# Joined products for both halves of the softmax weights, and the forget gate inside the value projection

## The chip, the core and the metric

The kernel runs on one core of one Trainium2 chip. The metric is the device time of one execution in microseconds (us), lower is better. Times below are medians of runs; the rows come from one more execution that the hardware profiler recorded.

## What is computed

One decoder layer over 2048 tokens of width 1024, in float32. Three sub-layers, each `x <- x + RMSNorm(f(RMSNorm(x)))`: a token mixer with a causal convolution (width 31) beside attention with a forget gate, a cross-attention to 256 memory tokens, and a squared-ReLU MLP of width 4096. The change touches the attention of the mixer:

```
log_f = log_sigmoid(f_logit + b_forget)            # 8 heads, one column each of the input projection
cum = cumsum(log_f, axis=1)
logits = q @ k.T * scale + cum[q] - cum[k]         # causal, 8 heads of 64, in blocks of 128 queries
p = softmax(logits)
out = p @ v
```

## The kernel before

A float32 product that must be exact enough is made of float32r parts: every operand `x` is split into a high half (a rounded copy, made by ACT) and a low half (`x - high`, made by DVE), and a product of two split operands takes three matmuls: high by high, high by low, low by high. `mm3` (lines 160 to 167) issues them; `split` (134) makes the halves; `weight` (144) loads a weight tile and splits it.

The tokens go through in four chunks of 512. `mix_in` (336) handles 1024 tokens (two chunks) at a time: the gated linear unit and the keys and queries of each 128 channels, and then the values, in two column halves `b` of 256 (four heads of 64 each), 128 tokens at a time. Results go to DRAM. `attend` (492) runs the attention of one chunk: 8 heads, each in two blocks of 256 queries. For a block, `scores` (539) makes the logits in pieces of up to 512 keys (line 560, 561), adds the bias and takes the row maximum on DVE, and exponentiates on ACT. `values` (580) then walks over the keys in pairs of 128: four transpositions on PE (line 594) of the weights into one PSUM bank `pt`, the split of it into `pp` (high by ACT, low by DVE, line 598), and, one pair behind, the products with the values (line 610) into `o`. The value tile holds, for 128 keys, 64 high and 64 low columns, so that one matmul yields 128 rows: `v_high` times the weights and `v_low` times the weights. Each key block takes two matmuls of 256 columns, one with the high half of the weights and one with the low; the second block of the last pair, which only 128 of the queries may see, takes 128 columns. At the end ACT copies one half of the rows of `o` and DVE adds the other (lines 616, 617).

The forget gate (`gate`, 458) is made early, after the first 128 channels of `mix_in`: 32 matmuls of 512 columns for each 1024 tokens (lines 467, 468) with a stationary operand of 40 columns, then a chain on ACT and DVE over tiles of 8 partitions by 1024 tokens, with a running sum over the tokens at its end. The sums go to DRAM (`dnc`), and `attend` reads them back for every head, spread over 128 partitions (`bias`).

What runs beside what: `drive` (932) interleaves two streams of work. The main stream is `mix_in` for the first and second 1024 tokens and then the four MLPs; the side stream is the attention, output projection and cross-attention of chunk 0, 1, 2, 3. The convolution (480 taps of `acc`, one DVE instruction each, and 16 first taps) comes from a background list between them; what is left of a chunk's taps when its output projection needs them is flushed. A scheduler then orders the instructions of every engine by priority, and the numbers in `SCHED` (57) set ratios and leads: `r0`, `a1`, `m0` to `m2` the share of side work, `a0`, `b1`, `bm` that of the convolution, `hw`, `hb`, `hs`, `hm` leads of weights, background, side and main.

Of the kernel before, what the change touches and what calls it, by code (L numbers as in the profile page):

```python
# [10 lines left out]
F32 = mybir.dt.float32  # L11
F32R = mybir.dt.float32r
# [6 lines left out]
P = 128  # L19
# [6 lines left out]
NH = 8  # L26
# [27 lines left out]

SCHED = dict(hw=135, hb=117, hs=62.8, hm=39.2, r0=0.243, a0=0.35, a1=1.16, b1=0.186, m0=0.85, m1=0.986, m2=1.12,
           bm=0.161, y1=3.05, y2=2.3, y3=2.97, y4=1.95)


class Engine:
# [19 lines left out]
class Trunk:  # L81
# [130 lines left out]
    def setup(self):  # L212
        nc, i = self.nc, self.i
        ct = lambda shape, name, dt=F32: self.cpool.tile(shape, dt, name=name)
        self.ident = ct([P, P], "ident")
        make_identity(nc, self.ident)
        self.ones = ct([P, 1], "ones")
        self.v.memset(self.ones, 1.0)
        self.mean_d, self.mean_c = ct([P, 1], "mean_d"), ct([P, 1], "mean_c")
        self.v.memset(self.mean_d, 1.0 / D)  # L220
        self.v.memset(self.mean_c, 1.0 / CCH)
        self.eps = ct([P, 1], "eps")
        self.v.memset(self.eps, EPS)
# [4 lines left out]
        self.bf = ct([NH, 1], "bf")  # L228
        self.wf = ct([P, KT, 32 + NH], "wf", F32R)
        self.carry = ct([NH, 1], "carry")  # L230
# [12 lines left out]
        self.d_x1 = [self.dram([P, KT, TC], name="dx1") for _ in range(NCH)]  # L243
        self.d_x2 = [self.dram([P, KT, TC], name="dx2") for _ in range(NCH)]

    def setup_late(self):
        nc, i = self.nc, self.i
        self.load(self.cw, i["conv_w"])
        self.load(self.cvec, i["cvec"])
        self.load(self.bf, i["b_forget"])  # L250
# [4 lines left out]
        self.v.memset(self.wf.bitcast(F32), 0.0)  # L255
        raw = self.tile("vs", [P, KT, NH], name="wfraw")
        self.load(raw, i["w_f"])
        yield 1
        self.a.copy(self.wf[:, :, 0:NH], raw)
        self.v.tensor_tensor(out=self.wf[:, :, 32 : 32 + NH], in0=raw,  # L260
                                in1=self.wf[:, :, 0:NH].bitcast(F32), op=ALU.subtract)


    def mem_load(self):
# [71 lines left out]
    def mix_in(self, h, ht, late, after):  # L336

        nc, i = self.nc, self.i
        for t in range(4):
            glu, key, query = self.glu(h, t, ht), self.qk(h, t, ht, 12), self.qk(h, t, ht, 8)  # L340
            if t == 0:
                for _ in range(4):
                    yield next(glu)
                next(late, None)
                yield next(key)
                for _ in late:
                    pass
                yield next(key)
            yield from glu
            yield from key  # L350
            yield from query
            if t == 0:
                yield from self.gate(h, ht)
        for b in range(2):
            wv = []
            for q in range(2):
                wv.append([self.tile("mu", [P, 4, 256], F32R, name="wv") for _ in range(2)])
                self.weight(i["w_v"][b, q], [4, 256], wv[q])
            wk = [(wv[k // 4][0][:, k % 4], wv[k // 4][1][:, k % 4]) for k in range(KT)]
            for t in range(8):  # L360
                sl = slice((t % 4) * P, (t % 4 + 1) * P)
                ps = self.ps("mm")
                self.mm3(ps[:, :256], [(a[:, sl], bb[:, sl]) for a, bb in ht[t // 4]], wk)
                v = self.tile("ms", [P, 4, 2, DH], F32R, name="v")
                pv = ps[:, :256].rearrange("p (h d) -> p h d", d=DH)
                self.split(v[:, :, 0], v[:, :, 1], pv)
                self.store(
                    self.d_v[h][4 * b : 4 * b + 4, :, t].rearrange("h p d -> p h d"),
                    v.bitcast(F32).rearrange("p h l d -> p h (l d)"))
                yield 2.6  # L370
                if b == 1 and t == 3:
                    for _ in after:
                        pass
# [81 lines left out]
                              scale=self.cvec[:, 1, t : t + 1])  # L455
            yield SCHED["y4"]

    def gate(self, h, ht):

        nc = self.nc  # L460
        W = HALF
        z, e, u, ln = [self.tile("mu", [NH, W], name="gate") for _ in range(4)]
        for j in range(2):
            ps = self.ps("mm")
            for k in range(KT):
                xh, xl = ht[j][k]
                nc.tensor.matmul(ps[: 32 + NH], self.wf[:, k], xh, start=k == 0, stop=False)
                nc.tensor.matmul(ps[: 32 + NH], self.wf[:, k], xl, start=False, stop=k == KT - 1)
            sl = slice(j * TC, (j + 1) * TC)
            self.a.copy(e[:, sl], ps[32 : 32 + NH])  # L470
            self.v.scalar_tensor_tensor(
                out=z[:, sl], in0=ps[:NH], scalar=self.bf, in1=e[:, sl], op0=ALU.add, op1=ALU.add)
            yield 3.5
# [4 lines left out]
        self.a.activation(ln, u, AF.Ln)  # L478
        self.v.reciprocal(u, u)
        self.mul(e, e, u)  # L480
        self.v.tensor_tensor(out=ln, in0=ln, in1=e, op=ALU.subtract)
        self.v.tensor_scalar(out=z, in0=z, scalar1=0.0, scalar2=None, op0=ALU.min)
        self.v.tensor_tensor(out=ln, in0=ln, in1=z, op=ALU.subtract)
        self.v.tensor_tensor_scan(
            out=u, data0=self.ones[:NH, 0:1].to_broadcast([NH, W]), data1=ln,
            initial=0.0 if h == 0 else self.carry, op0=ALU.mult, op1=ALU.add)
        if h == 0:
            self.a.copy(self.carry, u[:, W - 1 : W])
        self.store(self.d_nc[h], u)


    def attend(self, c):
# [87 lines left out]
    def values(self, c, hd, b, prow, v):  # L580
# [1 line left out]
        L = c * TC + (b + 1) * QB  # L582
        e = hd % 2
        nk = L // P
        o = self.ps("o")[:, :QB]
        prev = None
        for k0 in range(0, nk + 2, 2):
            cur = None
# [10 lines left out]
                cur = (k0, pp)  # L599
            if prev is not None:  # L600
                g, pp = prev
                order = [(0, 0), (0, 1), (1, 0), (1, 1)]
                if g == nk - 2:
                    order = [(0, 0), (1, 0), (1, 1), (0, 1)] if g == 0 else order[2:] + order[:2]
                for n, (k, l) in enumerate(order):
                    if g + k == nk - 1:
                        out, rhs = o[:, P:], pp[:, l, QB : QB + P]
                    else:
                        out, rhs = o, pp[:, l, k * QB : (k + 1) * QB]
                    nc.tensor.matmul(out, v[:, g + k], rhs, start=g == 0 and n == 0, stop=g == nk - 2 and n == 3)  # L610
# [473 lines left out]
```

## Time and profile before

| what | value |
|---|---|
| median of 3 runs | 2839.58 us (2838.35 to 2840.03) |
| the profiled execution: time, span | 2844.77 us, 2843.0 us |
| PE busy | 2774.1 us (98%), 13922 matmuls |
| DVE busy | 1966.3 us (69%) |
| ACT busy | 1380.7 us (49%) |
| POOL busy | 207.2 us (7%) |
| mean granted TensorE clock | 0.993 of full speed |

The profiled execution is 5.2 us (0.18%) above the median. Busy time is the time with at least one instruction of the engine in flight; matmuls overlap, so what one costs is read from the distance between the starts of neighbours. An idle stretch is put down to the instruction whose end released it.

### The profile page before, as it was taken

The numbers are of one execution on the slowest core, as the hardware profiler recorded it, in microseconds if no ns is written. First come the engines' busy times: TensorE is split into PE (matmuls) and PEld (weight loads), VectorE is DVE, ScalarE is ACT, GpSimd is POOL, SyncE is SP. The second block draws the span as 40 slices with busy tenths as digits, with TensorE's granted clock in tenths as the row PEclk, the third lists the DMA queues.
The fourth block names the chain that finished last, engine by engine and source line by source line (L and its number), as shares of the span: only waits on it lengthen the run. The fifth ranks groups of instructions, "written<-read, shape, count | busy, mean of one in ns | idle before, by whom it ended". The sixth has DMA issues, their size and how long they took to land.

```text
span 2843.0 us, 37221 instructions
## 1 busy us (share of the span) xinstructions
PE 2774.1 (98%) x13922; PEld 2303.9 (81%) x13922; DVE 1966.3 (69%) x3521; ACT 1380.7 (49%) x2164; POOL 207.2 (7%) x367
## 2 busy tenths in 40 slices
PE   7999999999999999989999999999999999999997
PEld 5889778888888887878888888878887888888887
DVE  8878896669787676888886645876665555844436
ACT  5333654345654445556554445655555445543332
POOL 0010300001110000021100001011100000000000
PEclk9999999999999999999999999999999999999999
DMA  5366645456544344456453435354524342342332
GB/s 170 116 221 167 172 131 164 141 163 199 153 135 130 128 136 145 149 151 175 133 147 115 149 107 167 127 180 146 151 93 135 119 148 97 130 145 97 97 96 82
DMA packets 141045, 398.32 MB, mean 140 GB/s; under 512 B 15248, under 2 KB 37904, under 8 KB 136000
## 3 DMA queue, kind: packets, MB, share of 16 engines
q1 hardware_dynamic: 99952, 262.40, 29.0%
q0 software_dynamic: 40912, 133.54, 16.3%
q8 instruction: 110, 1.80, 0.3%
q14 instruction: 71, 0.58, 0.1%
HBM read 330.68 MB, written 65.20 MB: 139 GB/s over the span
## 4 chain that ended last, share of the span: by engine, by line
PE 78%; DMA 5%; issue 5%; DVE 4%; ACT 2%; POOL 1%; SPq 0%; POOLq 0%; DVEq 0%; ACTq 0%
PE mm L165 17%; PE mm L166 17%; PE mm L167 17%; PE sc L167 4%; PE sc L165 4%; PE sc L166 4%; PE o L610 4%; PE pt L594 3%; PE sc L560 2%; PE sc L561 2%; DMA bias<-dnc 1%; DMA rb<-drs 1%; DMA cu<-du 1%; DVE yacc L73 1%; DVE acc L73 1%
## 5 line engine op out<-in xcount | busy, mean ns | idle before, releaser
L73 ACT CAST wh<-wr 128x1024 fp32r<-128x1024 f32 x282 | 296.5, 1052 | 705.6 <-PE mm L166 640.8
L165 PE MATMUL mm<-h,wh 128*128 128x512 f32 x1504 | 597.8, 398 | 6.2 <-ACT h L73 2.6
L166 PE MATMUL mm<-h,wh 128*128 128x512 f32 x1504 | 595.3, 396 | 1.7 <-DVE h L73 1.7
L167 PE MATMUL mm<-h,wl 128*128 128x512 f32 x1504 | 596.5, 397 | 0.0
L73 DVE TENSOR_TENSOR wl<-wr,wh 128x1024 fp32r<-128x1024 f32 x282 | 345.3, 1224 | 276.4 <-ACT wh L73 274.9
L165 PE MATMUL mm<-hid,wh 128*128 128x512 f32 x992 | 395.4, 399 | 0.6 <-DVE yacc L73 0.6
L167 PE MATMUL mm<-hid,wl 128*128 128x512 f32 x992 | 392.9, 396 | 0.0
L166 PE MATMUL mm<-hid,wh 128*128 128x512 f32 x992 | 392.1, 396 | 0.0
L73 DVE SCALAR_TENSOR_TENSOR acc<-cu,convw,acc 128x512 f32<-128x512 f32 x480 | 357.0, 748 | 5.9
L165 PEld LDWEIGHTS mm<-h,wh 128*128 128x128 f32 x1504 | 284.0, 189 | 65.7 <-ACT h L73 3.0
L166 PEld LDWEIGHTS mm<-h,wh 128*128 128x128 f32 x1504 | 283.9, 189 | 60.4 <-DVE h L73 3.2
L167 PEld LDWEIGHTS mm<-h,wl 128*128 128x128 f32 x1504 | 283.7, 189 | 58.1
L73 DVE TENSOR_TENSOR yacc<-mm,yacc 128x512 f32<-128x512 f32 (+1 forms) x232 | 154.9, 669 | 159.4 <-PE mm L167 158.1
L73 DVE TENSOR_TENSOR pp<-pt,pp 128x512 fp32r<-128x512 f32 (+1 forms) x288 | 186.8, 656 | 71.7 <-ACT pp L73 70.2
L73 ACT CAST pp<-pt 128x512 fp32r<-128x512 f32 (+1 forms) x288 | 159.4, 560 | 130.1 <-PE pt L594 123.7
L165 PEld LDWEIGHTS mm<-hid,wh 128*128 128x128 f32 x992 | 186.4, 188 | 39.9 <-DVE yacc L73 1.7
L167 PEld LDWEIGHTS mm<-hid,wl 128*128 128x128 f32 x992 | 186.5, 188 | 38.0 <-issue 0.5
L166 PEld LDWEIGHTS mm<-hid,wh 128*128 128x128 f32 x992 | 186.6, 188 | 36.8 <-DVE hid L73 0.2
L594 PE MATMUL pt<-ident,prow 128*128 128x128 f32 x1088 | 200.0, 276 | 3.5 <-ACT prow L73 3.5
L73 ACT ACTIVATE prow<-prow,mx 128x128 f32<-128x128 f32 (+15 forms) x128 | 154.2, 1205 | 79.9 <-DVE mx L73 77.2
L73 DVE CUSTOM_DVE_ANT_0 prow<-sc,bias 128x512 f32<-128x512 f32 (+3 forms) x288 | 166.8, 596 | 34.3 <-PE sc L561 29.5
L610 PE MATMUL o<-pp,vv 128*128 128x256 f32 (+1 forms) x832 | 179.7, 300 | 8.8 <-DVE pp L73 8.1
(234 smaller groups left out, 4569.4 us busy)
## 6 DMA issues: line engine op xcount, KB each, us to landing
wr<-in_w_up_dram SPq DMA_DIRECT2D x128, 512.0 KB, 3.6
wr<-in_w_down_dram SPq DMA_DIRECT2D x128, 512.0 KB, 3.5
wr<-in_w_in_dram SPq DMA_DIRECT2D x32, 512.0 KB, 4.2
q<-dq POOLq DMA_DIRECT2D x64, 256.0 KB, 5.7
wr<-in_w_out_dram SPq DMA_DIRECT2D x32, 512.0 KB, 3.5
dx<-y SPq DMA_DIRECT2D x16, 1024.0 KB, 4.2
bias<-dnc POOLq DMA_DIRECT2D x32, 512.0 KB, 5.7
x<-in_x_dram POOLq DMA_DIRECT2D x12, 1024.0 KB, 6.3
```

Of the source, the lines that this page charges most:

```text
L73: ins = op(*args, **kw)
L165: mm(ps, ah, bh, start=first and j == 0, stop=False)
L166: mm(ps, ah, bl, start=False, stop=False)
L167: mm(ps, al, bh, start=False, stop=last and j == n - 1)
L560: nc.tensor.matmul(ps[:, :w], q[:, 0, qs], ks[:, k0 : k0 + w], start=True, stop=False)
L561: nc.tensor.matmul(ps[:, :w], q[:, 1, qs], ks[:, k0 : k0 + w], start=False, stop=True)
L594: nc.tensor.transpose(pt[:, at : at + P], prow[t][:, (k0 + k) * P : (k0 + k + 1) * P], self.ident)
L610: nc.tensor.matmul(out, v[:, g + k], rhs, start=g == 0 and n == 0, stop=g == nk - 2 and n == 3)
```

## The change

It has three parts. First, `values` makes one matmul of each key block for both halves of the weights: the moving operand is the high and the low half side by side (512 columns), the result goes to two halves of the PSUM bank, and one more DVE addition joins them. The columns of the value tile are laid out so that the high half of the values stands on the same rows for both, and the product of the low halves is not added up any more. Second, the eight columns of the forget gate become columns 256 to 263 of the value projection's moving operand for the first four heads; the gate's chain then works on 128 partitions by 64, and the running sum is made by small matmuls with triangular constants. The chain comes at the end of the first half of the value projection. Third, eight numbers of `SCHED` differ, and the scheduler orders all engines anew.

```diff
-SCHED = dict(hw=135, hb=117, hs=62.8, hm=39.2, r0=0.243, a0=0.35, a1=1.16, b1=0.186, m0=0.85, m1=0.986, m2=1.12,
-           bm=0.161, y1=3.05, y2=2.3, y3=2.97, y4=1.95)
+SCHED = dict(hw=153, hb=124, hs=61, hm=42.2, r0=0.254, a0=0.346, a1=1.16, b1=0.186, m0=0.85, m1=0.986, m2=1.12,
+             bm=0.102, y1=3.12, y2=2.3, y3=2.97, y4=1.95)
...
+        for t in (self.tri, self.same, self.prior):
+            nc.gpsimd.memset(t, 1.0)
+        sel(self.tri, [[1, P]], 0, -1)
...
-            if t == 0:
-                yield from self.gate(h, ht)
...
-                wv.append([self.tile("mu", [P, 4, 256], F32R, name="wv") for _ in range(2)])
-                self.weight(i["w_v"][b, q], [4, 256], wv[q])
+                wv.append([self.tile("mu", [P, 4, 256 + NH], F32R, name="wv") for _ in range(2)])
+                self.weight(i["w_v"][b, q], [4, 256], [w[:, :, :256] for w in wv[q]])
+                for l in range(0 if b else 2):
+                    self.a.copy(wv[q][l][:, :, 256:], self.wf[:, l, 4 * q : 4 * q + 4])
...
-                self.mm3(ps[:, :256], [(a[:, sl], bb[:, sl]) for a, bb in ht[t // 4]], wk)
-                v = self.tile("ms", [P, 4, 2, DH], F32R, name="v")
-                pv = ps[:, :256].rearrange("p (h d) -> p h d", d=DH)
-                self.split(v[:, :, 0], v[:, :, 1], pv)
+                self.mm3(ps[:, :cols], [(a[:, sl], bb[:, sl]) for a, bb in ht[t // 4]], wk)
+                if b == 0:
+                    self.add(zs[0][:, t], ps[:, 256:cols], self.bf)
+                v = self.tile("ms", [P, 2, 4, DH], F32R, name="v")
+                pv = ps[:, :256].rearrange("p (g e d) -> p g e d", e=2, d=DH)
+                self.split(v[:, :, 0:4:3], v[:, :, 1:3], pv)
...
+                if b == 0 and t == 7:
+                    self.gate(h, zs)
...
-        for j in range(2):
-            ps = self.ps("mm")
-            for k in range(KT):
-                xh, xl = ht[j][k]
-                nc.tensor.matmul(ps[: 32 + NH], self.wf[:, k], xh, start=k == 0, stop=False)
-                nc.tensor.matmul(ps[: 32 + NH], self.wf[:, k], xl, start=False, stop=k == KT - 1)
...
-        self.v.tensor_tensor_scan(
-            out=u, data0=self.ones[:NH, 0:1].to_broadcast([NH, W]), data1=ln,
-            initial=0.0 if h == 0 else self.carry, op0=ALU.mult, op1=ALU.add)
...
-        self.store(self.d_nc[h], u)
+        n = NH * 8
+        ps = self.ps("stat")
+        nc.tensor.matmul(ps[:n, :P], ln.rearrange("p h t -> p (h t)"), self.tri, start=True, stop=True)
+        self.a.copy(cum, ps[:n, :P])
+        self.a.copy(self.tot[h], cum[:, P - 1 : P])
+        ps = self.ps("stat")
+        if h == 1:
+            nc.tensor.matmul(ps[:n, :1], self.same, self.tot[0], start=True, stop=False)
+        nc.tensor.matmul(ps[:n, :1], self.prior, self.tot[h], start=h == 0, stop=True)
+        off = self.st([n, 1], name="off")
+        self.a.copy(off, ps[:n, :1])
+        self.v.tensor_scalar(out=cum, in0=cum, scalar1=off, scalar2=None, op0=ALU.add)
+        self.store(self.d_nc[h].rearrange("h (t q) -> (h t) q", q=P), cum)
...
-        o = self.ps("o")[:, :QB]
+        o = self.ps("o").rearrange("p (l q) -> p l q", l=2)
...
-                order = [(0, 0), (0, 1), (1, 0), (1, 1)]
-                if g == nk - 2:
-                    order = [(0, 0), (1, 0), (1, 1), (0, 1)] if g == 0 else order[2:] + order[:2]
-                for n, (k, l) in enumerate(order):
-                    if g + k == nk - 1:
-                        out, rhs = o[:, P:], pp[:, l, QB : QB + P]
-                    else:
-                        out, rhs = o, pp[:, l, k * QB : (k + 1) * QB]
-                    nc.tensor.matmul(out, v[:, g + k], rhs, start=g == 0 and n == 0, stop=g == nk - 2 and n == 3)
+                every, late = slice(0, QB), slice(P, QB)
+                if g < nk - 2:
+                    order = [(0, every), (1, every)]
+                elif g > 0:
+                    order = [(1, late), (0, every)]
+                else:
+                    order = [(0, slice(0, P)), (0, late), (1, late)]
+                for n, (k, q) in enumerate(order):
+                    at = 0 if k == 0 else QB - q.start
+                    nc.tensor.matmul(o[:, :, q], v[:, g + k], pp[:, :, at + q.start : at + q.stop],
+                                     start=g == 0 and k == 0 and (n == 0 or nk == 2),
+                                     stop=g == nk - 2 and (n != 0 if g > 0 else n != 1))
...
-        self.a.copy(tmp[mine], o[other])
-        self.add(tmp[mine], o[mine], tmp[mine])
+        self.a.copy(tmp[mine], o[other, 0])
+        self.add(tmp[mine], o[mine, 0], tmp[mine])
+        self.add(tmp[mine], o[mine, 1], tmp[mine])
```

Two places of the engines' order show how the instructions move. The first is PE in the attention of the fourth chunk (last head, second block of queries, keys 1024 to 1279), before; `pt` holds transposed weights, `pp` their two halves, `o` the result, and `mm` the MLP's up and down products of the main stream. Here `pt_3327` becomes `pp_3328`:

```order
L594 MATMUL pt_3327_19030<-ident_66,prow_3281_18788 128x128
L594 MATMUL pt_3327_19030<-ident_66,prow_3282_18789 128x128
L610 MATMUL o_3318_18985<-pp_3326_19023,vv_3235_18555 128x256 x4
L594 MATMUL pt_3329_19042<-ident_66,prow_3281_18788 128x128
L594 MATMUL pt_3329_19042<-ident_66,prow_3282_18789 128x128
L594 MATMUL pt_3329_19042<-ident_66,prow_3281_18788 128x128
L594 MATMUL pt_3329_19042<-ident_66,prow_3282_18789 128x128
L610 MATMUL o_3318_18985<-pp_3328_19035,vv_3235_18555 128x256
L167 MATMUL mm_3336_19072<-hid_3199_18358,wl_3335_19069 128x512
L165 MATMUL mm_3336_19072<-hid_3221_18475,wh_3334_19068 128x512
L610 MATMUL o_3318_18985<-pp_3328_19035,vv_3235_18555 128x256 x3
```

The same place in the changed kernel, from right behind the last transposition of `pt_3323`, which becomes `pp_3324`:

```order
L631 MATMUL o_3314_18466<-pp_3322_18500,vv_3231_18057 128x512 x2
L613 MATMUL pt_3330_18549<-ident_66,prow_3277_18279 128x128
L166 MATMUL mm_3328_18521<-hid_3213_17962,wh_3326_18517 128x512
L613 MATMUL pt_3330_18549<-ident_66,prow_3278_18280 128x128
L167 MATMUL mm_3328_18521<-hid_3213_17962,wl_3327_18518 128x512
L613 MATMUL pt_3330_18549<-ident_66,prow_3277_18279 128x128
L165 MATMUL mm_3328_18521<-hid_3240_18085,wh_3326_18517 128x512
L613 MATMUL pt_3330_18549<-ident_66,prow_3278_18280 128x128
L166 MATMUL mm_3328_18521<-hid_3240_18085,wh_3326_18517 128x512
L167 MATMUL mm_3328_18521<-hid_3240_18085,wl_3327_18518 128x512
L165 MATMUL mm_3329_18535<-hid_3067_17272,wh_3326_18517 128x512
L631 MATMUL o_3314_18466<-pp_3324_18510,vv_3231_18057 128x512
```

Between the last transposition of a pair and its first product stood 8 matmuls, none of them of 512 columns; now there stand 12, eight of them of 512 columns. The first product needs both halves, where it needed the high one alone and the second needed the low one.

The second place is PE in the value projection of the first 1024 tokens, second column half, in the changed kernel. `stat_288` is the gate's running sum over 128 tokens, `stat_289` the sums of the blocks before it; nothing stood here before, the gate's 32 matmuls came some 1000 rows earlier:

```order
L167 MATMUL mm_301_2097<-wv_294_2028,h_82_226 128x256
L497 MATMUL stat_288_2012<-tri_88,gate_268_1728 64x128
L165 MATMUL mm_305_2132<-wv_291_2022,h_79_223 128x256
L166 MATMUL mm_305_2132<-wv_292_2023,h_79_223 128x256
L167 MATMUL mm_305_2132<-wv_291_2022,h_80_224 128x256
L165 MATMUL mm_305_2132<-wv_291_2022,h_79_223 128x256
L166 MATMUL mm_305_2132<-wv_292_2023,h_79_223 128x256
L503 MATMUL stat_289_2016<-tot0_86,prior_90 64x1
L167 MATMUL mm_305_2132<-wv_291_2022,h_80_224 128x256
```

`stat_288` stands 72 matmuls (three tiles of the value projection) behind the last tile that carries gate columns.

## Rows read from the trace of the kernel before

**Rows 1.** The page's first part: busy time, share, instructions of each engine.
```profile
PE 2774.1 (98%) x13922; PEld 2303.9 (81%) x13922; DVE 1966.3 (69%) x3521; ACT 1380.7 (49%) x2164; POOL 207.2 (7%) x367
```

**Rows 2.** Busy time by stretch; after DVE, ACT, POOL: granted clock, DMA share, GB/s.
```profile
0.00:40.00 40.00, 22.00 (x86) 17.19 (x87) 27.78 (x44) 22.83 (x33) 4.39 (x12) 1.00 0.54 182
190.00:400.00 210.00, 202.36 (x1158) 170.12 (x1157) 179.90 (x384) 111.06 (x204) 33.82 (x61) 0.99 0.62 172
600.00:800.00 200.00, 196.76 (x1200) 171.75 (x1198) 155.95 (x361) 110.95 (x201) 28.97 (x52) 0.98 0.60 175
1200.00:1400.00 200.00, 191.24 (x1053) 159.68 (x1052) 172.95 (x403) 124.34 (x199) 35.65 (x64) 0.97 0.53 152
1800.00:2000.00 200.00, 193.07 (x1086) 162.34 (x1085) 150.51 (x364) 124.88 (x190) 28.86 (x53) 0.97 0.47 144
2000.00:2200.00 200.00, 197.73 (x1070) 162.88 (x1069) 130.03 (x262) 110.80 (x160) 15.63 (x27) 1.00 0.42 128
2800.00:2843.00 43.00, 28.68 (x217) 26.83 (x215) 32.05 (x84) 10.51 (x24) 0.00 (x0) 0.86 0.18 62
```

**Rows 3.** PE in order of time: start, duration; matmuls of 512, 256 columns, the gate's.
```profile
1000.81 0.39 PE L166 MATMUL mm<-h,wh 128*128 128x512 f32 x1
...
1003.08 0.39 PE L167 MATMUL mm<-h,wl 128*128 128x512 f32 x1
...
261.72 0.28 PE L165 MATMUL mm<-wv,h 128*128 128x256 f32 x1
...
262.80 0.28 PE L165 MATMUL mm<-wv,h 128*128 128x256 f32 x1
...
71.65 0.40 PE L467 MATMUL mm<-h,wf 128*40 128x512 f32 x1
...
76.96 0.39 PE L468 MATMUL mm<-h,wf 128*40 128x512 f32 x1
```

**Rows 4.** Groups by line and shape, PE at line 610: busy, mean ns | idle before.
```profile
L610 PE MATMUL o<-pp,vv 128*128 128x256 f32 x768 | 172.8, 304 | 8.7 <-DVE pp L73 8.1 <-ACT pp L73 0.4
L610 PE MATMUL o<-pp,kv 128*128 128x256 f32 x256 | 59.1, 304 | 2.2 <-ACT pp L73 0.8 <-DVE pp L73 0.7 <-DVE otmp L73 0.3
```

**Rows 5.** In order of time, fourth chunk's attention: transpositions, split, products of one pair.
```profile
2133.42 0.60 PE L594 MATMUL pt<-ident,prow 128*128 128x128 f32 x4
...
2133.77 0.71 PE L610 MATMUL o<-pp,vv 128*128 128x256 f32 x4
...
2134.05 0.59 ACT L73 CAST pp<-pt 128x512 fp32r<-128x512 f32 x1 [1.65 <-PE pt L594]
...
2134.33 0.60 PE L594 MATMUL pt<-ident,prow 128*128 128x128 f32 x4
...
2134.67 0.69 DVE L73 TENSOR_TENSOR pp<-pt,pp 128x512 fp32r<-128x512 f32 x1 [1.17 <-ACT pp L73]
2134.69 0.39 PE L610 MATMUL o<-pp,vv 128*128 128x256 f32 x1
...
2135.42 0.62 PE L610 MATMUL o<-pp,vv 128*128 128x256 f32 x3
```

**Rows 6.** In order of time, DVE and PE: the two longest waits of an attention.
```profile
1275.95 0.69 DVE L73 TENSOR_TENSOR yacc<-yacc,x2r 128x512 f32<-128x512 f32 x1 [4.47 <-DMA x2r<-dx]
...
1277.97 0.84 PE L610 MATMUL o<-pp,vv 128*128 128x256 f32 x3 [4.33 <-DVE pp L73]
...
1886.94 0.79 PE L560 MATMUL sc<-ks,q 128*128 128x512 f32 x1 [4.70 <-DVE mx L73]
```

**Rows 7.** Groups by line and shape on DVE: taps, joining of `o`, the gate's reciprocal.
```profile
L73 DVE SCALAR_TENSOR_TENSOR acc<-cu,convw,acc 128x512 f32<-128x512 f32 x480 | 357.0, 748 | 5.9
...
L73 DVE TENSOR_TENSOR otmp<-o,otmp 64x256 f32<-64x256 f32 x64 | 26.9, 421 | 15.6 <-ACT otmp L73 14.3
...
L73 DVE RECIPROCAL gate<-gate 8x1024 f32<-8x1024 f32 x2 | 13.1, 6532 | 0.0
```

More of the change, by code (lines that the diff above doesn't have):

```diff
@@ L227, in setup @@
         self.cvec = ct([P, 3, 4], "cvec")
-        self.bf = ct([NH, 1], "bf")
-        self.wf = ct([P, KT, 32 + NH], "wf", F32R)
-        self.carry = ct([NH, 1], "carry")
+        self.bf = ct([P, NH], "bf")
+        self.wf = ct([P, 2, KT, NH], "wf", F32R)
+        self.tot = [ct([NH * 8, 1], f"tot{h}") for h in range(2)]
+        self.tri = ct([P, P], "tri")
+        self.same, self.prior = [ct([NH * 8, NH * 8], n) for n in ("same", "prior")]
         self.rs = {c: ct([P, NH, 4], f"rs{c}") for c in range(NCH)}
@@ L249, in setup_late @@
         self.load(self.cvec, i["cvec"])
-        self.load(self.bf, i["b_forget"])
+        self.load(self.bf, i["b_forget"].rearrange("h o -> o h").to_broadcast([P, NH]))
         z = self.tile("vs", [P, PAD], name="zpad")
@@ L258, in setup_late @@
         yield 1
-        self.a.copy(self.wf[:, :, 0:NH], raw)
-        self.v.tensor_tensor(out=self.wf[:, :, 32 : 32 + NH], in0=raw,
-                                in1=self.wf[:, :, 0:NH].bitcast(F32), op=ALU.subtract)
+        self.split(self.wf[:, 0], self.wf[:, 1], raw)
+        n = NH * 8
+        sel = lambda t, pattern, base, cm: nc.gpsimd.affine_select(
+            out=t, in_=t, pattern=pattern, compare_op=ALU.is_ge, fill=0.0, base=base, channel_multiplier=cm)
+        for t in (self.tri, self.same, self.prior):
+            nc.gpsimd.memset(t, 1.0)
+        sel(self.tri, [[1, P]], 0, -1)
+        sel(self.prior, [[1, n]], -1, -1)
+        for t in (self.same, self.prior):
+            t = t.rearrange("p (h t) -> p h t", t=8)
+            sel(t, [[-8, NH], [0, 8]], 0, 1)
+            sel(t, [[8, NH], [0, 8]], 7, -1)
     def mem_load(self):
@@ L356, in mix_in @@
             for q in range(2):
-                wv.append([self.tile("mu", [P, 4, 256], F32R, name="wv") for _ in range(2)])
-                self.weight(i["w_v"][b, q], [4, 256], wv[q])
-            wk = [(wv[k // 4][0][:, k % 4], wv[k // 4][1][:, k % 4]) for k in range(KT)]
+                wv.append([self.tile("mu", [P, 4, 256 + NH], F32R, name="wv") for _ in range(2)])
+                self.weight(i["w_v"][b, q], [4, 256], [w[:, :, :256] for w in wv[q]])
+                for l in range(0 if b else 2):
+                    self.a.copy(wv[q][l][:, :, 256:], self.wf[:, l, 4 * q : 4 * q + 4])
+            cols = 256 if b else 256 + NH
+            wk = [(wv[k // 4][0][:, k % 4, :cols], wv[k // 4][1][:, k % 4, :cols]) for k in range(KT)]
+            if b == 0:
+                buf = self.tile("ms", [P, 4 * 8 * NH + P], name="gate")
+                zs = [buf[:, 64 * j : 64 * j + 64].rearrange("p (t h) -> p t h", h=NH) for j in range(3)]
+                zs += [buf[:, 192:256].rearrange("p (h t) -> p h t", t=8), buf[: NH * 8, 256 : 256 + P]]
             for t in range(8):
@@ L362, in mix_in @@
                 ps = self.ps("mm")
-                self.mm3(ps[:, :256], [(a[:, sl], bb[:, sl]) for a, bb in ht[t // 4]], wk)
-                v = self.tile("ms", [P, 4, 2, DH], F32R, name="v")
-                pv = ps[:, :256].rearrange("p (h d) -> p h d", d=DH)
-                self.split(v[:, :, 0], v[:, :, 1], pv)
+                self.mm3(ps[:, :cols], [(a[:, sl], bb[:, sl]) for a, bb in ht[t // 4]], wk)
+                if b == 0:
+                    self.add(zs[0][:, t], ps[:, 256:cols], self.bf)
+                v = self.tile("ms", [P, 2, 4, DH], F32R, name="v")
+                pv = ps[:, :256].rearrange("p (g e d) -> p g e d", e=2, d=DH)
+                self.split(v[:, :, 0:4:3], v[:, :, 1:3], pv)
                 self.store(
                     self.d_v[h][4 * b : 4 * b + 4, :, t].rearrange("h p d -> p h d"),
-                    v.bitcast(F32).rearrange("p h l d -> p h (l d)"))
+                    v.bitcast(F32).rearrange("p g (e l) d -> p (g e) (l d)", e=2))
                 yield 2.6
+                if b == 0 and t == 7:
+                    self.gate(h, zs)
                 if b == 1 and t == 3:
@@ L456, in conv_norm, with gate @@
             yield SCHED["y4"]
-    def gate(self, h, ht):
+    def gate(self, h, z):
         nc = self.nc
-        W = HALF
-        z, e, u, ln = [self.tile("mu", [NH, W], name="gate") for _ in range(4)]
-        for j in range(2):
-            ps = self.ps("mm")
-            for k in range(KT):
-                xh, xl = ht[j][k]
-                nc.tensor.matmul(ps[: 32 + NH], self.wf[:, k], xh, start=k == 0, stop=False)
-                nc.tensor.matmul(ps[: 32 + NH], self.wf[:, k], xl, start=False, stop=k == KT - 1)
[L469 to L473, printed above, removed]
+        z, e, u, ln, cum = z
+        lt = ln.rearrange("p h t -> p t h")
         self.a.activation(e, z, AF.Abs)
@@ L477, in gate @@
         self.v.scalar_tensor_tensor(out=e, in0=u, scalar=-1.0, in1=e, op0=ALU.add, op1=ALU.subtract)
-        self.a.activation(ln, u, AF.Ln)
+        self.a.activation(lt, u, AF.Ln)
         self.v.reciprocal(u, u)
         self.mul(e, e, u)
-        self.v.tensor_tensor(out=ln, in0=ln, in1=e, op=ALU.subtract)
+        self.v.tensor_tensor(out=lt, in0=lt, in1=e, op=ALU.subtract)
         self.v.tensor_scalar(out=z, in0=z, scalar1=0.0, scalar2=None, op0=ALU.min)
-        self.v.tensor_tensor(out=ln, in0=ln, in1=z, op=ALU.subtract)
-        self.v.tensor_tensor_scan(
-            out=u, data0=self.ones[:NH, 0:1].to_broadcast([NH, W]), data1=ln,
-            initial=0.0 if h == 0 else self.carry, op0=ALU.mult, op1=ALU.add)
-        if h == 0:
-            self.a.copy(self.carry, u[:, W - 1 : W])
-        self.store(self.d_nc[h], u)
+        self.v.tensor_tensor(out=lt, in0=lt, in1=z, op=ALU.subtract)
+        n = NH * 8
+        ps = self.ps("stat")
[10 more added lines that the diff above has]
+        self.store(self.d_nc[h].rearrange("h (t q) -> (h t) q", q=P), cum)
     def attend(self, c):
```

1 line of the change is left out of this document (removed).

## The prediction

> **What bounds the kernel.** I read the page first, then stretches of time, then single matmuls. PE is busy 98% of the span, DVE 69%, ACT 49% [rows 1]: whatever leaves PE's queue shortens the kernel unless PE then waits for somebody. So I need three things of PE: what a matmul costs, where PE waits, and on whom.
>
> A matmul's drawn duration overlaps the next, so its cost is the distance between starts. Ten steps of 512 columns take 2.27 us, 0.227 us each; nine of 256 columns take 1.08 us, 0.120 us each; the gate's 23 steps take 5.31 us, 0.231 us each [rows 3]. For 128 columns I take half of the 256, 0.06 us.
>
> The waits lie in the stretches that hold an attention [rows 2]. The four of 190 to 400, 600 to 800, 1200 to 1400 and 1800 to 2000 us leave PE idle for 7.6, 3.2, 8.8 and 6.9 us, 26.5 us together. Their granted clock is 0.99, 0.98, 0.97, 0.97, so some 2 + 4 + 6 + 6 = 18 us more are lost while PE runs at the lower of its two levels (1.2 instead of 2.4 GHz) behind a wait. The start (18 us idle before 40 us) and the end (14 us idle after 2800 us) have nothing to do with this change. DVE is busy 86% of the first and of the third of these stretches: there PE's lead over DVE is thin.
>
> Beside the idle time there are waits too short to show. In [rows 5] four transpositions of a pair start at 2133.42 and are over by 2133.77; ACT ends the high half at 2134.64, DVE the low half at 2135.36. That is 1.6 us, and PE had eight matmuls (0.92 us) and two of the main stream before the three remaining products could start at 2135.42. No idle time is booked, because a product is drawn 0.28 us long and the next of its kind is due after 0.12 us.
>
> **The change, part by part.** The sum is made against the profiled execution (2844.77 us) and then taken off the median, 2839.58 us; the two differ by 0.18%, which changes none of the terms.
>
> 1. Joined products. Before: 1024 of 256 columns [rows 4] and, by the code, 128 of 128 columns: 1024 x 0.120 + 128 x 0.06 = 130.6 us. After, counted in the order: 504 of 512 columns and 80 of 2 x 128: 504 x 0.227 + 80 x 0.120 = 124.0 us. That is -6.6 us, all of it on PE's queue.
>
> That two matmuls of 256 columns cost 0.013 us more than one of 512 is what the rows show. The Trainium skill, TensorE: Matmul & The Clock Gate, section Back-to-back issue gap, gives less to be had: 262 cycles at 256 columns and 518 at 512, so 0.0025 us a pair. By it this term, as an estimate, would be about -1.4 us and the forecast 5 us later; the measured distances decide.
>
> 2. Gate. 64 matmuls go: 64 x 0.231 = -14.8 us. 384 matmuls of the value projection grow from 256 to 264 columns; the rows give (0.227 - 0.120) / 256 = 0.42 ns a column, so 384 x 8 x 0.42 ns = +1.3 us. Five small matmuls come (two of 128 columns in plain float32, three of one column). No row shows these; between 0.06 and 0.23 us each, the upper end by the 512-column row, they are 0.3 to 1.2 us; I take +1.0, being unsure of the float32 ones.
>
> Sum of PE's work: -6.6 - 14.8 + 1.3 + 1.0 = **-19.1 us**.
>
> 3. Waits before the products. The first product now needs both halves, and the scheduler puts it later: in the order, 8 matmuls between became 12 at the place shown, eight of them of 512 columns, and the median over all 288 pairs goes from 12 to 15. Valuing the matmuls by the distances above (and a transposition at the 0.11 us that the eight in [rows 5] leave for it), 83 pairs had less than 1.4 us of PE's work between, and 7 have now. The split alone takes 0.59 + 0.69 = 1.28 us [rows 5]. For the short waits of those pairs 83 x 0.16 = 13 us is the upper bound (0.16 is what a 0.28 us product hides), zero the lower; I take -8. Of the 10.9 us idle before products [rows 4], 4.33 us belong to a load: DVE sat 4.47 us on the landing of `x2r`, the low half behind it, PE behind that [rows 6]. That stays, as does the like wait of 4.70 us before the logits at 1886.94. Of the other 6.6 us I take -5, and -2 of the 18 us of lower clock: together **-15 us**, between 0 and -35 (all four stretches' idle time but these two waits, and the clock with it).
>
> 4. New wait: the gate's chain now ends late. Its first small matmul stands in PE's in-order queue 72 matmuls (72 x 0.12 = 8.6 us) behind the last tile with gate columns. In between lie three ACT and seven DVE instructions of the chain, with other work between: three taps at 0.748 us [rows 7], splits, table loads. If the chain is late, the value projection queued behind waits on PE; then `dnc` must land before `bias` of chunk 0 can be loaded, and DVE's first logits of that chunk wait for it, with the next value splits behind them. For two halves I take +3 us, between 0 and +10.
>
> 5. DVE. 64 more joins cost 64 x 0.421 = 27 us [rows 7], seven a chunk. The gate's long chain goes, its reciprocal alone 13.1 us [rows 7], the rest of like size, so DVE's total stays. But its place moves. Counted in the order, the second attention holds 29 taps of the convolution instead of 40, the third 39 instead of 58, and the fourth 43, where it had none: 43 x 0.748 + 16 x 0.421 = 39 us. Its stretch 1800 to 2200 us has DVE busy 280.5 of 400 us [rows 2], so 320 after, 80%, still under the 86% of the third. I take +3 us, between -3 and +10. The rest of the reorder (weights led in earlier, `hm`, `r0`) I cost at nothing: main products between the attentions run at 0.227 us without gaps, and their cover is two weight buffers of 5.4 us each; without it a late weight would cost what the wait before it costs.
>
> Sum: -19.1 - 15 + 3 + 3 = -28.1, so 2839.58 - 28.1 = **2811 us**.
>
> **The rivals.** *Waits only move* (0.22): DVE is what is late where it is 86% busy; then a later product just lets the logits or transpositions wait instead. For it: the two longest waits are DVE's. Only the work leaves: 2839.6 - 19.1 + 6 = 2826 us. *Waits go for good* (0.12): the lower clock follows the waits, so it goes with them: -35 instead of -15, which makes 2839.6 - 19.1 - 35 + 6 = 2791 us; against it, the load of `x2r` stays. *The gate is late* (0.08): +10 instead of +3 in term 4: 2818 us; for it, the 8.6 us of lead against a chain of ten steps in two busy queues.
>
> *Slower: the joined product does not run at 0.227 us* (0.06). Its moving operand is read in two runs of 256 columns, and the 80 late ones write two runs of 128; no row of before has such a shape. It decides at 28 us / 504 = 0.056 us each, that is from 0.283 us a product on. The upper end is 0.39 us, as long as a 512-column matmul is drawn [rows 3], with nothing overlapped; halfway, at 0.31 us, 504 x 0.083 = 42 us come back, and the time is 2853 us. Against it: the 512-column products of the main stream use the same engine and width, and runs of 256 are long. PSUM — Partial Sum Buffer of the Trainium skill, section Specifications (TRN2), says that any non-contiguous access pattern slows matmuls significantly; no run here shows how much, and the full joined products write the bank without a gap.
>
> **How the numbers follow.** Forecast as summed: 0.52. The range takes in the moved waits on one side and nearly all of the lasting gain on the other, with the bounds of terms 3 to 5: 2790 to 2834 us. A measurement of this kernel tells about 0.2% (5.7 us) from no change. Faster needs less than 2833.9 us: forecast, the two waits rivals and the late gate, 0.52 + 0.22 + 0.12 + 0.08 less a little for their upper ends: 0.90. The same: 0.04. Slower: the joined product's case, 0.06.
>
> **What would show it.** In the profile after: products of 512 columns start 0.227 us after their predecessor's kind (else term 1 is wrong); no 40-column matmuls, 264-column ones 0.123 us apart; PE's idle time before products below 6 us; granted clock in the attention stretches 0.98 or better; the small matmuls waiting under 2 us each for DVE or ACT; DVE near 80% in the fourth attention with idle PE no more than before. If the idle time before logits and transpositions grows by what the products lose, the first rival holds; if PE stands before `stat` or DVE before the first `bias`, the third.

## The result, and the profile after

The changed kernel takes 2820.27 us (median, 2818.8 to 2820.73) against 2839.81 us of the kernel before, timed beside it: ratio 0.9929, 95% interval [0.9912, 0.9947], so 19.5 us less. The forecast was 2811 us, the range 2790 to 2834. The profiled executions differ by more, 2843.0 against 2818.8 us of span, because that of before lay 5 us above its median.

The page's first part, to be read against [rows 1]: PE has 622 matmuls and 28 us less, DVE as much as before.

```profile
PE 2745.9 (97%) x13300; PEld 2255.2 (80%) x13300; DVE 1962.6 (70%) x3596; ACT 1372.1 (49%) x2171; POOL 206.1 (7%) x376
```

Busy time by stretch, the columns of [rows 2]:

```profile
0.00:40.00 40.00, 21.11 (x86) 16.57 (x87) 27.31 (x43) 22.69 (x33) 6.15 (x21) 1.00 0.54 178
190.00:400.00 210.00, 200.45 (x1120) 170.79 (x1119) 180.21 (x407) 112.47 (x211) 34.17 (x62) 0.98 0.59 165
600.00:800.00 200.00, 194.10 (x1110) 164.82 (x1108) 156.91 (x393) 118.40 (x217) 29.75 (x52) 0.98 0.53 164
1200.00:1400.00 200.00, 190.14 (x963) 153.66 (x962) 165.42 (x397) 120.50 (x194) 37.36 (x69) 0.98 0.57 160
1800.00:2000.00 200.00, 195.13 (x999) 156.49 (x998) 172.13 (x403) 123.00 (x187) 31.88 (x57) 1.00 0.52 156
2000.00:2200.00 200.00, 196.67 (x947) 157.33 (x946) 134.34 (x255) 101.58 (x146) 12.63 (x23) 1.00 0.39 123
```

PE is idle for 9.6, 5.9, 9.9 and 4.9 us in the four stretches of an attention, 30.2 us together, where it was 26.5. The granted clock is a little better. Idle time has not fallen there, so the gain has to be looked for elsewhere.

PE in order of time, two places (start, duration): joined products, then 264-column matmuls, as in [rows 3, 5].

```profile
2045.20 0.39 PE L166 MATMUL mm<-h,wh 128*128 128x512 f32 x1
2045.42 0.62 PE L631 MATMUL o<-pp,vv 128*128 128x512 f32 x2
2045.88 0.60 PE L613 MATMUL pt<-ident,prow 128*128 128x128 f32 x4
...
228.74 0.28 PE L167 MATMUL mm<-wv,h 128*128 128x264 f32 x1
...
230.07 0.28 PE L166 MATMUL mm<-wv,h 128*128 128x264 f32 x1
```

Two joined products take 0.46 us (2045.42 to 2045.88), 0.23 each; eleven steps of 264 columns take 1.33 us, 0.121 each. The groups of the products by shape (busy, mean ns | idle before), answering [rows 4]:

```profile
L631 PE MATMUL o<-pp,vv 128*128 128x512 f32 x384 | 133.1, 411 | 5.1 <-DVE pp L73 4.9
L631 PE MATMUL o<-pp,kv 128*128 128x512 f32 x120 | 41.9, 409 | 1.7 <-DVE pp L73 1.7
L631 PE MATMUL o<-pp,kv 128*128 128x256 f32 x48 | 11.6, 295 | 0.0
L631 PE MATMUL o<-pp,vv 128*128 128x256 f32 x32 | 9.8, 307 | 1.2 <-DVE pp L73 1.2
```

The idle time before products is 8.0 us; it was 10.9, and I had said under 6. What PE waits for (us in total, times, longest), after:

```profile
PE sc L578 <- DMA ks<-dk: 8.6, 6, 4.2
PE o L631 <- DVE pp L73: 7.8, 11, 1.5
PE stat L182 <- DVE ss L73: 5.9, 2, 4.9
```

and before:

```profile
PE o L610 <- DVE pp L73: 8.9, 9, 4.3
PE sc L560 <- DVE mx L73: 4.9, 2, 4.7
```

The two long waits of [rows 6], 4.3 and 4.7 us, are gone, also from the logits, where I had let it stand. Two of the same size are new: 4.2 us for a load of keys and 4.9 us for a statistic.

**How lost time is counted below.** Idle time leaves out the short waits that a drawn duration hides. So I took all distances between starts of PE's matmuls and subtracted what each costs undisturbed (0.2267 us for 512 columns, 0.1233 for 264, 0.119 for 256, 0.06 for 128, 0.11 for a transposition). The sum of the prices is called work, the rest lost time, put down to the matmul that starts late. It has the lower clock in it too. Two things limit it. The first transposition of a row mostly starts 0.316 us after a 512-column matmul, and what follows the last one starts 0.028 us after it (medians, before); counted with a flat 0.11, this moves several us between transpositions and the matmuls behind them. And the joined products are priced at 0.2267 us, but undisturbed they take 0.231 (step 1 of the account below): against the kernels without them, theirs then have some 3 us more of work and as much less of lost time than the table says.

### The profile page after: what moved, and what is told of

The parts are those of the page before. It is cut to its first block, busy times and chain, and to the rows that moved or that the text cites. A ratio compares the mean times of both kernels' runs of the same rounds, so it can differ in the third digit from the quotient of the medians.

```text
span 2818.8 us, 36129 instructions
## 1 busy us (share of the span) xinstructions
PE 2745.9 (97%) x13300; PEld 2255.2 (80%) x13300; DVE 1962.6 (70%) x3596; ACT 1372.1 (49%) x2171; POOL 206.1 (7%) x376
## 4 chain that ended last, share of the span: by engine, by line
PE 87%; DMA 5%; DVE 4%; issue 2%; ACT 2%; POOL 0%; SPq 0%; DVEq 0%; POOLq 0%; ACTq 0%
PE mm L166 20%; PE mm L165 20%; PE mm L167 20%; PE sc L167 4%; PE sc L165 4%; PE sc L166 4%; PE o L631 4%; PE pt L613 4%; PE sc L578 2%; PE sc L579 2%; DMA rb<-drs 1%; DMA ks<-dk 1%; DVE yacc L73 1%; DMA x2r<-dx 1%; PE stat L182 1%
## 5 line engine op out<-in xcount | busy, mean ns | idle before, releaser
L613 PEld LDWEIGHTS pt<-ident,prow 128*128 128x128 f32 x1088 | 139.7, 141 | 33.0 <-ACT prow L73 3.9
```

Source lines behind the costliest of these rows:

```text
L613: nc.tensor.transpose(pt[:, at : at + P], prow[t][:, (k0 + k) * P : (k0 + k + 1) * P], self.ident)
```

## The experiments

**Which part brings it.** The change has three parts: joined products, the gate, and the table of interleaving numbers (`SCHED`). Every combination was timed; the first four are these, each with a line or two of its edit.

```diff
 parts_only: after
-SCHED = dict(hw=153, hb=124, hs=61, hm=42.2, r0=0.254, a0=0.346, ...
+SCHED = dict(hw=135, hb=117, hs=62.8, hm=39.2, r0=0.243, a0=0.35, ...
 sched_only: before, the two lines the other way round
 joined_only: before
...
+                    nc.tensor.matmul(o[:, :, q], v[:, g + k], pp[:, :, at + q.start : at + q.stop],
 gate_only: before
...
+                wv.append([self.tile("mu", [P, 4, 256 + NH], F32R, name="wv") for _ in range(2)])
...
```

Expected of `parts_only` (both edits of the program, old table):

> Both edits of the program (joined products, gate in the value projection), but with the old table of interleaving numbers. PE's work by the recorded terms is -19 us against the kernel before, as in the changed kernel. Theory 1 (the waits taken from the products come back before other matmuls, whatever the interleaving): 2820 us, within 3 us of the changed kernel. Theory 2 (the products' waits are really gone, and the new table gives them back): 2805 to 2812 us, faster than the changed kernel by 8 us or more. Theory 3 (the edits made new waits and the new table takes them away): 2826 to 2834 us.

Of `sched_only`:

> The kernel before with the new table of interleaving numbers and nothing else; PE's work is the same. Theory 1: 2840 us within 4. Theory 2 (the new table costs some 10 us by itself): 2847 to 2855 us. Theory 3 (the new table is better by itself): 2830 us or less.

Of `joined_only`:

> The kernel before with the joined products alone (layout of the value tile, products, the second join), the old gate and the old table. Recorded terms: work -6.6 us, waits before products -15, conv taps and joins +3. If both of the first terms hold: about 2820 us. Theory 1 (only the work leaves): 2833 us, within 3. If the joined product cost as its width alone says, 0.0025 us a pair: 2838 us. In the profile the idle time before products should fall below 6 us in either case, and by theory 1 the idle time before logits, loads and statistics grows by as much.

Of `gate_only`:

> The kernel before with the gate moved into the value projection alone, old products and old table. Recorded terms: work -14.8 + 1.3 + 1.0 = -12.5 us, late gate chain +3: about 2830 us. Theory 1 (work alone): 2827 us, within 3. If the chain behind the last gate columns is late at its upper bound: 2837 us, with PE idle before the triangular matmul. If the gate's waits before were larger than I saw, below 2822 us.

The other two combinations take the changed kernel and undo one edit, under the new table. Expected of `joined_sched` (no gate edit):

> The changed kernel without the gate's edit: joined products, old gate, new table of numbers, hidden tiles 4096 bytes apart. Theory 1 (each order lands within some 12 us of its work, whatever part is in it; the new table was found for the whole): work -6 us, so 2834 us, and anywhere from 2825 to 2846. Theory 2 (the new table suits the joined products): the waits fall as in the changed kernel and the hidden products are at 389 ns, so 2820 us + 12 of work - 10 of the buffers' place = 2822 us, within 4.

Of `gate_sched` (no joined products):

> The changed kernel without the joined products: gate in the value projection, new table of numbers. Theory 1 (each order lands within some 12 us of its work): work -12 us, hidden products +10, so 2838 us, and anywhere from 2828 to 2850; the old table gave 2852. Theory 2 (the new table suits the joined products): no better than with the old table, 2848 to 2856 us. Theory 3 (the new table suits the gate): 2826 us, the changed kernel and the 6 us of the products.

Ratios to the kernel before, with their intervals, and, from one profiled execution each, work and lost time of PE in us, with some of the places where it is lost. Three of these executions lay away from their kernel's median, which is in the lost time: the kernel before 5 us above it, the new table alone 8 us above, both edits under the old table 4 us below.

```
joined gate table | ratio  [95%]            | work   lost | products logits statistics hidden tiles
  -     -    old  | 1                       | 2690.2 131.0|  33.6     22.9     7.6       2.6
  -     -    new  | 1.0007 [0.9997, 1.0017] | 2690.2 137.6|  30.7     20.2    13.2       2.8
 yes    -    old  | 1.0037 [1.0024, 1.0050] | 2684.4 140.0|  22.3     27.7     7.4       2.6
 yes    -    new  | 1.0006 [0.9994, 1.0018] | 2684.4 133.6|  19.4     21.5     9.8       2.7
  -    yes   old  | 1.0042 [1.0028, 1.0056] | 2677.7 151.3|  22.4     41.3    14.6       9.2
  -    yes   new  | 1.0000 [0.9986, 1.0013] | 2677.7 137.6|  33.6     23.1    18.5       9.4
 yes   yes   old  | 0.9997 [0.9985, 1.0009] | 2671.9 140.1|  19.0     34.4    15.2       9.4
 yes   yes   new  | 0.9929 [0.9912, 0.9947] | 2671.9 124.8|  19.1     30.3    15.0       9.7
```

Each edit alone, under the old table, makes the kernel slower, by 10.5 and 12 us (0.0037 and 0.0042 of 2840), although the work falls by 6 and 12.5 us. Both together under the old table change nothing. The table alone changes nothing either. Only the three together gain 20 us. Read the other way, each part has four neighbours that differ by it alone:

- joined products: +10.5, -0.3, -12.8, -20.2 us, on the average -5.7;
- gate: +11.9, -2.0, -11.4, -21.9 us, on the average -5.8;
- table: +2.0, -8.8, -11.9, -19.3 us, on the average -9.5.

The average of the joined products is near their work, the gate's is not. Either may be chance with four numbers so far apart; the scatter itself is the finding. Of the first four expectations only `sched_only`'s first theory came out (2843 us); none had either edit of the program make the kernel slower. The other two runs fit their first theory, that each order lands within some 12 us of its work, and not that the new table suits one part alone. A single pair of kernels can't price a part of 6 us here.

Still, the lost time says where joining acts. Before the products it falls in all four pairs, by 11.3, 11.3, 3.4 and 14.5 us (a recount with the two starts at transpositions allowed for gives 12.2, 10.8, 2.8 and 14.6; with the flat price the fall from before to after is only 8.6). Before the logits it rises in three of them, by 4.8, 1.3 and 7.2, and falls by 6.9 in the third pair. The lost time as a whole goes +9.0, -4.0, -11.2 and -12.8. So what leaves the products comes back in part elsewhere, and how much depends on the order.

**Hidden tiles.** In the last column, every kernel with the gate's edit loses 7 us more at matmuls that have nothing to do with it: those of the MLP with a tile of `hid` as moving operand. The widened `wv` tile shares its five rotating buffers with `hid`, and a buffer is as large as its largest tile. `pad_only` makes them larger and does nothing else; the instructions and their order on PE, DVE, ACT and POOL are in its trace those of the kernel before.

```diff
-                wv.append([self.tile("mu", [P, 4, 256], F32R, name="wv") for _ in range(2)])
+                wv.append([self.tile("mu", [P, 4 * 264], F32R, name="wv")[:, :1024].rearrange("p (k n) -> p k n", k=4)
+                           for _ in range(2)])
```

> The kernel before with one thing changed: the tile of the value weights is 128 bytes a partition longer, so the five buffers that it shares with the MLP's hidden tiles stand 4224 instead of 4096 bytes apart, as in the changed kernel. No instruction is added, removed or moved. In the traces the products of hidden tiles last 393 ns (median) wherever the gate stands in the value projection, and 389 ns elsewhere; started 231 instead of 228 ns apart, 2976 of them make 10 us. Theory 1 (the buffers' place does it): the hidden products at 393 ns and 2847 to 2852 us. Theory 2 (it comes from something else in the gate's edit): 389 ns and 2840 us within 3.

Measured: 2847.14 us against 2840.72, ratio 1.0024 [1.0013, 1.0034], so 6.8 us slower. The tile's own matmuls in the profile (duration ns min/median/max, first and last start), in the kernel before, in `pad_only` and in the changed kernel:

```profile
L165 PE MATMUL mm<-hid,wh x992: 387/389/499, 739.0 to 2784.7; 128*128 128x512 f32 x199
```
```profile
L165 PE MATMUL mm<-hid,wh x992: 387/393/501, 738.2 to 2789.2; 128*128 128x512 f32 x199
```
```profile
L165 PE MATMUL mm<-hid,wh x992: 387/393/793, 725.0 to 2761.3; 128*128 128x512 f32 x199
```

Three such lines, 2976 matmuls, have a median of 393 ns instead of 389. The lost time at undisturbed hidden matmuls goes from 2.6 to 9.6 us in `pad_only`, as its time does. Theory 1 holds: the buffers' place does it. It is not a matter of PE in general: successive main-stream matmuls that move `h` start 0.227 us apart (median) in all three kernels.

**One number, the smallest step.** `step_hm` and `bm_back` each take the changed kernel and turn one number of the table.

```diff
 step_hm
-SCHED = dict(hw=153, hb=124, hs=61, hm=42.2, ...
+SCHED = dict(hw=153, hb=124, hs=61, hm=43.2, ...
 bm_back
-             bm=0.102, y1=3.12, ...
+             bm=0.161, y1=3.12, ...
```

> The changed kernel with the smallest step of a single number: the main stream's lead goes from 42 to 43. No work changes. Theory 1 (the number fits this order alone; each other order lands some 5 to 20 us higher): 2825 to 2840 us. Theory 2 (the gain of the table is a matter of where its numbers lie roughly, as of the ratio between the streams): 2820 us within 4.

> The changed kernel with one number of the table back at its old value, the one that paces the convolution's taps: the four attentions hold 23, 44, 61 and 0 taps again, where the changed kernel has 23, 31, 40 and 43. No work changes. My prediction's step 5 (taps in the fourth attention cost): 2815 us or less. Theory 1 (any step from the table lands some 5 to 20 us higher): 2825 to 2840. Theory 3 (the taps' place is what the table gains by): 2835 to 2840, and the lost time in the second and third attention up by 10 us or more.

`step_hm`: 2827.15 us, ratio 0.9950 [0.9932, 0.9968], some 6 us over the changed kernel; the two intervals overlap, so this only leans to theory 1. `bm_back`: 2821.72 us against 2841.93, ratio 0.9937 [0.9924, 0.9951], the changed kernel's time. No theory there expected that: turning this number is no loss, 43 taps in the fourth attention cost nothing that shows (my step 5), and the table's gain isn't in their place. Which of its other numbers bring it stays open.

**A wait removed.** In the changed kernel PE stands for the mean of squares of the first chunk. PE in order of time:

```profile
652.25 0.28 PE L167 MATMUL mm<-wv,h 128*128 128x256 f32 x1
657.39 1.87 PE L182 MATMUL stat<-mean_d,ss 128*128 128x1 f32 x8 [4.86 <-DVE ss L73]
659.12 0.56 PE L578 MATMUL sc<-kv,q 128*128 128x256 f32 x1
```

The statistic isn't needed for a long time. `late_mean` puts it two tiles of the value projection later.

```diff
                 if b == 1 and t == 3:
+                    for _ in range(8):
+                        next(after, None)
+                if b == 1 and t == 5:
                     for _ in after:
                         pass
...
+            if behind:
+                self.tc.keep_in_program_order(ins)
```

> The changed kernel with one statistic later: the four small matmuls of the first chunk's mean of squares, at which PE stands 4.9 us for DVE in the changed kernel, wait two tiles of the value projection longer; their result is needed only at the end of that chunk's MLP. Nothing else of the work changes, and the order is the same before and nearly so behind. Theory of the sum (a wait removed in one place comes off the time): 2815 us, within 2. Theory of moving waits (the 4.9 us come back before what DVE delivers next): 2820 us within 2.

Measured: 2823.69 us against 2841.93, ratio 0.9937 [0.9925, 0.9950]; nothing is gained. PE in order of time at the same place:

```profile
655.59 0.28 PE L167 MATMUL mm<-wv,h 128*128 128x256 f32 x1
660.95 0.58 PE L583 MATMUL sc<-kv,q 128*128 128x256 f32 x1 [5.08 <-DVE mx L73]
```

PE now passes the statistic and stands 5.08 us at the logits, for DVE again. The stretch 640 to 665 us (columns as above), in the changed kernel and in `late_mean`:

```profile
640.00:665.00 25.00, 19.38 (x126) 17.46 (x125) 23.06 (x57) 16.14 (x33) 2.16 (x4) 0.86 0.46 151
```
```profile
640.00:665.00 25.00, 19.14 (x131) 17.18 (x131) 23.16 (x56) 17.66 (x33) 2.16 (x4) 0.87 0.51 177
```

DVE is busy for 23.1 and 23.2 of 25 us. By that it is the bound there, and the wait moves to the next thing that DVE delivers. This is the mechanism of my first rival, seen in one wait.

**Repairing the buffers' place.** `slots` holds the widened weights in three pairs of tiles, the third in the side stream's weight buffers, so that the hidden tiles stand 4096 bytes apart again. The value weights lie in DRAM in another order for that, and ACT has one more split. `slots_late` has the later statistic as well.

```diff
-            for q in range(2):
-                wv.append([self.tile("mu", [P, 4, 256 + NH], F32R, name="wv") for _ in range(2)])
...
+            for k0, n, tags in (((0, 4, ("mu", "mu")), (4, 4, ("mu", "mu"))) if b else
+                                ((0, 3, ("mu", "mu")), (3, 3, ("mu", "mu")), (6, 2, ("xh", "xl")))):
+                w = [self.tile(tag, [P, n, cols], F32R, name="wv") for tag in tags]
...
```

> The changed kernel with the value weights of its first half in three pairs of tiles (three, three and two blocks of rows) instead of two: the third pair lies in the side stream's weight buffers, and the hidden tiles stand 4096 bytes apart again. PE's work is the same, ACT has one more split and two more small copies. If the buffers' place costs what the padded kernel before showed (6.6 us by the clock, 7 by the distances of the matmuls): the hidden products at 389 ns and 2813 us, within 4 (the order between 190 and 670 us changes a little with the third pair). If it costs nothing here: 2820 us.

> Both of the last two edits together. If both hold and add up: 2808 us, within 4, 1.1% under the kernel before. If only the buffers' place counts: 2813 us.

`slots`: 2821.58 us, ratio 0.9936 [0.9921, 0.9951]. `slots_late`: 2824.29 us, 0.9945 [0.9929, 0.9961]. Neither beats the changed kernel. The hidden matmuls are as before the change (the first line of the tile in `slots`), and the statistic's wait is longer:

```profile
L165 PE MATMUL mm<-hid,wh x992: 387/389/791, 732.6 to 2760.4; 128*128 128x512 f32 x199
```
```profile
663.99 1.23 PE L182 MATMUL stat<-mean_d,ss 128*128 128x1 f32 x5 [9.23 <-DVE ss L73]
```

Lost time at hidden matmuls falls by 6.8 us (9.7 to 2.9), and that between 590 and 800 us rises by 8.0 (16.7 to 24.7). In the value projection of the second 1024 tokens the third pair changes the order, and DVE ends the statistic at 664 instead of 657 us. In `slots_late` the 9.2 us reappear at the logits, 9.4 us (in total, times, longest):

```profile
PE sc L585 <- DVE mx L73: 11.5, 5, 9.4
```

So this edit pays for its gain with another order where DVE is the bound; the repair without that price was not found.

## Why the prediction came out as it did

The time lay in the range, 9 us over the forecast, and the direction was right. Step by step it is right in part only.

1. **Joined products, -6.6 us.** Right in sign, too large in size. Nothing like 0.283 us shows, so the rival on the other side fell. But I took the distance of the main stream's matmuls for that of the products. Where nothing holds up the next matmul, a joined product takes 0.231 us (median of the 419 of 504 that are followed after 0.20 to 0.26 us), and one of 256 columns 0.118 (before, 752 of 1024, after 0.10 to 0.15). That saves 0.005 us a pair and not 0.013, so the part's work is about -2.6 us; the -5.8 of the table keeps my price. By the page of the Trainium skill named in the prediction (TensorE: Matmul & The Clock Gate, section Back-to-back issue gap) the joining would have left about 1.4 us, as an estimate. The trace lies nearer to that than to my 6.6, though each matmul takes more here than the page's 262 and 518 cycles, which are 0.109 and 0.216 us at 2.4 GHz.
2. **Gate, -12.5 us on PE.** Held for its own instructions: -12.5 us of work in the traces, no 40-column matmul, 0.121 us for 264 columns. The step that failed is "384 matmuls of the value projection grow from 256 to 264 columns": I priced the columns and not the tile. The larger tile moves five buffers, and the MLP pays 7 us for it (`pad_only`).
3. **Waits before products, -15 us.** The mechanism held at its place: from before to after 14.5 us of lost time leave the products (33.6 to 19.1), though by short waits more than by idle time, which fell by 2.9 and not 5. What failed is to let this come off the time. The logits lose 7.4 us more and the statistics 7.4, some of it in the two new long waits. The rival "waits only move" names the mechanism, and `late_mean` shows it for one wait. Its time, 2826 us, is not right either. One reading of mine was wrong, without weight for the sum: in [rows 5] the transpositions are drawn until 2134.02 us and not 2133.77, so the split came 1.34 us behind them and not 1.6.
4. **Late gate, +3 us.** Of the right size: by distances, the triangular matmul starts 1.67 us late in the first half and 0.68 in the second, each under the 2 us that I gave. The other half of the term, a wait for the chain's result in DRAM, doesn't show on DVE: it stands 1.7 us for `bias` after and 2.9 before. In the first half the profile books 1.51 us of PE's wait:

```profile
261.99 0.40 PE L497 MATMUL stat<-tri,gate 128*64 128x128 f32 x2 [1.51 <-DVE gate L73]
```

5. **DVE, +3 us.** DVE is busy 306.5 of 400 us from 1800 to 2200 us, 77%, near the 80% I gave, and `bm_back`, which takes the taps out again, gains nothing. The term is zero as far as these runs can tell.
6. **The reorder, "cost at nothing".** This failed most. With both edits in, the new table is worth 19.3 us; with the old one the same program is no faster than before.

The balance, on the medians: -19.5 us measured, of which work -18.3 and hidden tiles +7, so all waits together give some -8. With the joined products at their measured distance the work is -15, and the waits give -11.5. My terms 3 to 5 sum to -9. The number came close, but for another reason than I gave: under the old table the same work and hidden tiles make -8 to -11 us and the time doesn't move, so there the waits take 7 to 10 us back. The waits' gain belongs to the order found for the whole, and not to the later product as such. The 9 us by which I missed are the hidden tiles' 7 and 4 too many in term 1, less 2.5 that the waits gave beyond my terms; that these partly cancel is luck.

A part of term 3 came from a single execution 5 us above its median. I had written that this changes no term; of waits, which are 26 us of idle time in all, 5 us are much.

## What to carry to other kernels

Where a scheduler orders the work, a part taken alone is measured together with an order that was not set for it, and here that is worth as much as the parts (10 us against 6): price a part by its instructions, and time it under several orders before believing a single pair. Take a wait away only after looking at the engine that it waits for: at 92% busy it will be late for the next thing instead. And when a tile in a set of shared rotating buffers grows, look at the instructions of all other tiles in that set.

## What was not expected of the hardware

The same 512-column matmul takes 0.228 us from the one before with hidden tiles 4096 bytes apart and 0.231 us with 4224. By the sizes in the program, the five buffers then start 0, 128, 256, 384 and 512 bytes (modulo 4096) behind the first, where before all five start at the same place. In the changed kernel the mean distances are 229.5 ns for one of the five buffers and 231.3 to 231.6 for the other four; before, they are 227.8 to 228.1 for all. So the place of the moving operand's buffers counts for 1.5%. That even the buffer with 229.5 ns is slower than before was not explained, and the traces carry no addresses that would tell which one it is. Whether the weights' place, the writes of other engines, or the distance of the two halves decides was not tried.
